# A rotary embedding kernel: another order of the first small loads on the SyncE and ScalarE queues

## The chip, the cores and the metric

The kernel runs on one core of one Trainium2 chip. The metric is device time in microseconds (us) of one execution; lower is better. The kernel before was timed three times.

## The reference

`x` has the shape (8, 2048, 16, 64): batch, sequence, heads, head dimension, in float32. `cos` and `sin` have the shape (2048, 32), one row for each place in the sequence, and hold for all batches and heads. Each head's 64 values are taken as two halves and rotated:

```python
x1 = x[..., :head_dim // 2]
x2 = x[..., head_dim // 2:]
out1 = x1 * cos - x2 * sin
out2 = x1 * sin + x2 * cos
return concatenate([out1, out2], axis=-1)      # float32
```

In bytes: 67.1 MB of `x` are read, 67.1 MB are written, and sine and cosine are 256 KB each.

## The kernel before

**Layout.** The 2048 places are spread over 128 partitions, 16 in a row on each (`J` = 16), so that one partition has for each batch 16 rows of 1024 values (`W` = 16 heads x 64). Work is done in float16: loads on the GpSimd queue turn float32 into float16 on the way, and stores on it turn it back. `buf` holds five batches (`SLOTS` = 5), and batch b lives in slot b modulo 5.

**Queues.** Nearly all traffic goes through one queue, that of GpSimd (POOL), by the helper `queue` (line 57), which ties each transfer behind the one before it in program order. The calls from line 100 on are thus the order of the queue: load of batch 0 without its first two rows, store of the first row of batch 0, load of batches 1 and 2, load of batches 3 and 4, store of the rest of batch 0, store of 1 and 2, load of 5, load of 6 and 7, and so on. A store waits for VectorE's last step on its rows; a load into a used slot waits for the store that empties it.

**The opening.** SyncE (SP) asks for sine (line 50, `sin_f`). ScalarE (ACT) asks for cosine (line 51, `cos_f`) and then for the *head*: the first two rows of batch 0, 1 MB in float32 (line 52). The head isn't converted on its way; it lands in float32 in the space of slot 4. Then ScalarE works in program order:

- lines 101 and 102: two conversions of sine to float16, one of them with a minus sign (`sin_h`), ahead of which the table load of ScalarE runs;
- line 103: the conversion of cosine (`cos_h`);
- line 96, twice (`narrow_head`): the head's two rows to float16.

**The rotation.** `rotate` is three VectorE instructions: the swapped halves times sine into `v` (line 87), the values times cosine in place (line 91), and their sum (line 93). The first call takes the first row alone (128 x 1024 values), the second the other 15 rows of batch 0, and the others a whole batch each (128 x 16384).

**The end.** The last two rows of batch 7 are turned to float32 on ScalarE (line 127) and stored from SyncE (line 128), behind a part of the batch's store.

Of the kernel before, what the change touches and what calls it, by code (L numbers as in the profile page):

```python
# [1 line left out]

# [4 lines left out]


@with_exitstack  # L10
def kernel(
    ctx: ExitStack,
    tc: tile.TileContext,
    x: bass.AP,
    cos: bass.AP,
    sin: bass.AP,
    out: bass.AP,
):
    nc = tc.nc
    f16 = mybir.dt.float16  # L20
    f32 = mybir.dt.float32

    B, S, H, D = x.shape
    Dh = D // 2
    P = nc.NUM_PARTITIONS
    J = S // P
    SLOTS = 5
    JA = 2
    JE = 2
    JF = 1  # L30

    pool = ctx.enter_context(tc.tile_pool(name="rope", bufs=1))
    buf = pool.tile([P, SLOTS, J, H, D], f16)
    v = pool.tile([P, J, H, D], f16)
    sin_f = pool.tile([P, J, Dh], f32)
    cos_f = pool.tile([P, J, Dh], f32)
    cos_h = pool.tile([P, J, Dh], f16)
    sin_h = pool.tile([P, J, D], f16)

    def words(slot, rows):  # L40
        flat = buf[:, slot, 0 : 2 * rows].rearrange("p j h d -> p (j h d)")
        return flat.bitcast(f32)

    head = words(SLOTS - 1, JA)
    tail = words(SLOTS - 2, JE)
    rows_in = x.rearrange("b (p j) h d -> p b (j h d)", j=J)
    rows_out = out.rearrange("b (p j) h d -> p b (j h d)", j=J)
    W = H * D

    nc.sync.dma_start(out=sin_f, in_=sin.rearrange("(p j) d -> p j d", j=J))  # L50
    nc.scalar.dma_start(out=cos_f, in_=cos.rearrange("(p j) d -> p j d", j=J))  # L51
    nc.scalar.dma_start(out=head, in_=rows_in[:, 0, 0 : JA * W])

    ring = []

    def queue(dst, src):
        dma = nc.gpsimd.dma_start(out=dst, in_=src)  # L57
        if ring:
            tc.add_manual_dep(
                dma.ins,  # L60
                ring[-1].ins.name,
                mybir.DependencyInfo(mybir.DependencyClass.NoSync, mybir.DependencyReason.DATA),
                reason="order of the ring",
            )
        ring.append(dma)
        return dma

    def part(b, n, j0, j1):
        s = b % SLOTS
        return buf[:, s : s + n, j0:j1].rearrange("p n j h d -> p n (j h d)")  # L70

    def load(b, n=1, j0=0):
        return queue(part(b, n, j0, J), rows_in[:, b : b + n, j0 * W : J * W])

    def store(b, n=1, j0=0, j1=J):
        return queue(rows_out[:, b : b + n, j0 * W : j1 * W], part(b, n, j0, j1))

    def rotate(b, j0=0, j1=J):
        n = j1 - j0
        js = slice(j0, j1)  # L80
        xt = buf[:, b % SLOTS, js]
        vt = v[:, js]
        shape = [P, n, H, 2, Dh]
        sin_b = sin_h[:, js, :].rearrange("p j (e d) -> p j e d", e=2).unsqueeze(2).to_broadcast(shape)
        cos_b = cos_h[:, js, :].unsqueeze(2).to_broadcast([P, n, 2 * H, Dh])
        xe = xt.rearrange("p j h (e d) -> p j h e d", e=2)
        nc.vector.tensor_mul(  # L87
            out=vt.rearrange("p j h (e d) -> p j h e d", e=2), in0=xe[:, :, :, ::-1, :], in1=sin_b
        )
        xw = xt.rearrange("p j h (e d) -> p j (h e) d", d=Dh)  # L90
        nc.vector.tensor_mul(out=xw, in0=xw, in1=cos_b)  # L91
        xa = xt.rearrange("p j h d -> p (j h d)")
        nc.vector.tensor_add(out=xa, in0=xa, in1=vt.rearrange("p j h d -> p (j h d)"))  # L93

    def narrow_head(j0, j1):
        nc.scalar.copy(  # L96
            out=buf[:, 0, j0:j1].rearrange("p j h d -> p (j h d)"), in_=head[:, j0 * W : j1 * W]
        )

    load(0, j0=JA)  # L100
    nc.scalar.copy(out=sin_h[:, :, Dh:D], in_=sin_f)  # L101
    nc.scalar.mul(out=sin_h[:, :, 0:Dh], in_=sin_f, mul=-1.0)  # L102
    nc.scalar.copy(out=cos_h, in_=cos_f)  # L103
    narrow_head(0, JF)
    narrow_head(JF, JA)
    rotate(0, 0, JF)
    store(0, j1=JF)
    load(1, 2)
    load(3, 2)
    rotate(0, JF, J)  # L110
    store(0, j0=JF)
    rotate(1)
    rotate(2)
    store(1, 2)
    load(5)
    load(6, 2)
    rotate(3)
    rotate(4)
    store(3, 2)
    rotate(5)  # L120
    rotate(6)
    store(5, 2)
    rotate(7)
    gate = store(7, j1=9)
    store(7, j0=9, j1=J - JE)

    nc.scalar.copy(out=tail, in_=buf[:, (B - 1) % SLOTS, J - JE : J].rearrange("p j h d -> p (j h d)"))  # L127
    end = nc.sync.dma_start(out=rows_out[:, B - 1, (J - JE) * W : J * W], in_=tail)
    tc.add_manual_dep(
        end.ins,  # L130
        gate.ins.name,
        mybir.DependencyInfo(mybir.DependencyClass.Sync, mybir.DependencyReason.DATA),
        reason="the last rows go out behind this part",
    )


# [1 line left out]
_INS = ['x', 'cos', 'sin']  # L138
_OUTS = [((8, 2048, 16, 64), 'float32')]


# [23 lines left out]
```

## Time and profile before

| | us |
|---|---|
| median of 3 runs (316.36 to 316.49) | 316.48 |
| the profiled execution, its own time | 316.32 |
| its span in the profile | 314.6 |
| VectorE (DVE) busy | 209.1 (66%) |
| ScalarE (ACT) busy | 6.8 (2%) |
| GpSimd (POOL) busy | 7.9 (3%) |
| HBM read and written over the span | 428 GB/s |
| head: from its issue at 1.15 to its landing | 12.1 |
| load of batch 0: from its issue at 1.25 to its landing | 22.6 |

The span is the stretch from the first to the last instruction that the profiler recorded; the execution's own time has some 1.7 us more around it. All places in time below are counted from the span's start. DVE, ACT, POOL and SP are the engines; a "q" behind a name (ACTq, SPq) is the engine's sequencer, which issues the transfers. q0 is GpSimd's queue, q1 SyncE's and q10 ScalarE's; all of them are served by the same 16 DMA engines. "Idle before" is time in which an engine waited, and the releaser is what ended it. A row of the timeline gives start and duration, then engine, line, operation, what is written and what is read, and in brackets the wait ahead of it.

### The profile page before, as it was taken

To read this page: it belongs to the slowest core of one execution; us is meant where nothing else is said; L and a number is where in the kernel's file an instruction comes from. 1 tells how busy PE (TensorE), PEld (TensorE's weight loads), DVE (VectorE), ACT (ScalarE), POOL (GpSimd) and SP (SyncE) were. 2 spreads that over 40 slices of the span, in tenths; PEclk is the share of its full clock that TensorE was granted. 3 is DMA by queue.
4 is the path that set the end of the run, shared out by engine and by line. 5 is a ranking of instruction groups with operands and counts; after the bars stand their busy time and mean duration, and the time that the engine had idled before them with its cause. 6 is when DMAs were issued, how large, how long until landed. Compare 5 with 4: busy or idle time off the path is not lost.

```text
span 314.6 us, 113 instructions
## 1 busy us (share of the span) xinstructions
DVE 209.1 (66%) x27; ACT 6.8 (2%) x7; POOL 7.9 (3%) x16
## 2 busy tenths in 40 slices
DVE  0109991089999999999994399903999999200000
ACT  3200000000000000000000000000000000200000
POOL 1020000000000000000000000000000000100000
DMA  7989999999999899999999999999999999999998
GB/s 230 261 193 249 267 200 200 200 267 200 200 200 325 375 500 400 400 400 533 400 200 221 246 200 200 250 217 333 400 517 417 400 400 525 408 400 400 433 425 342
DMA packets 3072, 101.71 MB, mean 323 GB/s; under 512 B 256, under 2 KB 256, under 8 KB 640
## 3 DMA queue, kind: packets, MB, share of 16 engines
q0 software_dynamic: 2496, 99.09, 98.1%
q1 hardware_dynamic: 288, 1.31, 1.2%
q10 hardware_dynamic: 288, 1.31, 1.0%
HBM read 67.63 MB, written 67.11 MB: 428 GB/s over the span
## 4 chain that ended last, share of the span: by engine, by line
DVE 59%; DMA 19%; another core or an unknown queue 7%; ACT 1%; issue 0%; POOL 0%; ACTq 0%; DVEq 0%
DVE v L87 20%; DVE buf L91 20%; DVE buf L93 20%; DMA buf<-in_x_dram 19%; ACT buf L127 1%; ACT buf L96 0%; POOL out_dram L57 0%; ACTq L51 0%; DVEq L87 0%
## 5 line engine op out<-in xcount | busy, mean ns | idle before, releaser
L87 DVE TENSOR_TENSOR v<-buf,sin_h 128x16384 f16<-128x16384 f16 (+2 forms) x9 | 69.7, 7744 | 59.7 <-DMA buf<-in_x_dram 45.3
L91 DVE TENSOR_TENSOR buf<-buf,cos_h 128x16384 f16<-128x16384 f16 (+2 forms) x9 | 69.7, 7744 | 0.3
L93 DVE TENSOR_TENSOR buf<-buf,v 128x16384 f16<-128x16384 f16 (+2 forms) x9 | 69.7, 7744 | 0.3
L57 POOL DMA_DIRECT2D out_dram<-buf x7 | 4.3, 620 | 219.7 <-DVE buf L93 219.7
L127 ACT CAST buf<-buf 128x2048 f32<-128x2048 f16 x1 | 1.9, 1897 | 254.2 <-DVE buf L93 254.2
L57 POOL DMA_DIRECT2D buf<-in_x_dram x5 | 3.4, 679 | 43.0 <-DMA out_dram<-buf 42.2
L96 ACT CAST buf<-buf 128x1024 f16<-128x1024 f32 x2 | 2.0, 1042 | 7.2 <-DMA buf<-in_x_dram 7.2
L101 ACT ACT_TABLE_LOAD x1 | 1.3, 1283 | 1.7 <-PEq L149 1.7
L101 ACT CAST sin_h<-sin_f 128x512 f16<-128x512 f32 x1 | 0.6, 617 | 1.5 <-DMA sin_f<-in_sin_dram 1.5
L102 ACT ACTIVATE sin_h<-sin_f 128x512 f16<-128x512 f32 x1 | 0.6, 624 | 0.0
L103 ACT CAST cos_h<-cos_f 128x512 f16<-128x512 f32 x1 | 0.6, 601 | 0.0
L149 POOL MEMSET const-float32-0.0<- 128x1 f32 x1 | 0.1, 99 | 0.2 <-issue 0.2
L149 POOL MEMSET const-bfloat16-1.0<- 128x1 bf16 x1 | 0.1, 102 | 0.0
L149 POOL MEMSET const-float32-1.0<- 128x1 f32 x1 | 0.1, 99 | 0.0
L149 POOL MEMSET const-uint8-127<- 128x1 uint8 x1 | 0.1, 99 | 0.0
## 6 DMA issues: line engine op xcount, KB each, us to landing
buf<-in_x_dram POOLq DMA_DIRECT2D x3, 8192.0 KB, 57.1
out_dram<-buf POOLq DMA_DIRECT2D x1, 7680.0 KB, 71.7
out_dram<-buf POOLq DMA_DIRECT2D x1, 4608.0 KB, 35.5
buf<-in_x_dram POOLq DMA_DIRECT2D x1, 4096.0 KB, 57.3
buf<-in_x_dram POOLq DMA_DIRECT2D x1, 3584.0 KB, 22.6
out_dram<-buf POOLq DMA_DIRECT2D x1, 2560.0 KB, 41.0
buf<-in_x_dram ACTq DMA_DIRECT2D x1, 1024.0 KB, 12.1
out_dram<-buf SPq DMA_DIRECT2D x1, 1024.0 KB, 8.4
```

What stands on the lines that cost most here:

```text
L57: dma = nc.gpsimd.dma_start(out=dst, in_=src)
L87: nc.vector.tensor_mul(out=vt.rearrange("p j h (e d) -> p j h e d", e=2), in0=xe[:, :, :, ::-1, :], in1=sin_b)
L91: nc.vector.tensor_mul(out=xw, in0=xw, in1=cos_b)
L93: nc.vector.tensor_add(out=xa, in0=xa, in1=vt.rearrange("p j h d -> p (j h d)"))
L96: nc.scalar.copy(out=buf[:, 0, j0:j1].rearrange("p j h d -> p (j h d)"), in_=head[:, j0 * W : j1 * W])
L101: nc.scalar.copy(out=sin_h[:, :, Dh:D], in_=sin_f)
L102: nc.scalar.mul(out=sin_h[:, :, 0:Dh], in_=sin_f, mul=-1.0)
L103: nc.scalar.copy(out=cos_h, in_=cos_f)
L127: nc.scalar.copy(out=tail, in_=buf[:, (B - 1) % SLOTS, J - JE : J].rearrange("p j h d -> p (j h d)"))
L149: nc = _bacc.Bacc("TRN2", target_bir_lowering=False, num_devices=1)
```

## The change

SyncE asks for sine and then for the head. VectorE clears one word of a new small tile, ScalarE copies it to the word beside it, and ScalarE's issue of cosine waits by semaphore for that copy. The copy is now ScalarE's first arithmetic instruction, so the table load comes ahead of it. All that follows is as it was.

```diff
     nc.sync.dma_start(out=sin_f, in_=sin.rearrange("(p j) d -> p j d", j=J))
-    nc.scalar.dma_start(out=cos_f, in_=cos.rearrange("(p j) d -> p j d", j=J))
-    nc.scalar.dma_start(out=head, in_=rows_in[:, 0, 0 : JA * W])
+    nc.sync.dma_start(out=head, in_=rows_in[:, 0, 0 : JA * W])
+    word = pool.tile([P, 2], f32)
+    nc.vector.memset(word[:, 0:1], 0.0)
+    warm = nc.scalar.copy(out=word[:, 1:2], in_=word[:, 0:1])
+    cosine = nc.scalar.dma_start(out=cos_f, in_=cos.rearrange("(p j) d -> p j d", j=J))
+    tc.add_manual_dep(
+        cosine.ins,
+        warm.ins.name,
+        mybir.DependencyInfo(mybir.DependencyClass.Sync, mybir.DependencyReason.DATA),
+        reason="the first rows are asked for ahead of cosine",
+    )
```

## The prediction

> **What bounds the kernel now.** I read the page first, then the chain of waits, then the timeline and the DMA view of the first microseconds, and last the trace's list of DMA packets, which has the queue, size, start and duration of each one (numbers called "packet" below are from that list, in microseconds from the span's start). From the page:
>
> ```profile
> span 314.6 us, 113 instructions
> ...
> DMA  7989999999999899999999999999999999999998
> ...
> q0 software_dynamic: 2496, 99.09, 98.1%
> q1 hardware_dynamic: 288, 1.31, 1.2%
> q10 hardware_dynamic: 288, 1.31, 1.0%
> ```
>
> The reader is to see that the packets of the three queues fill 100.3% of 16 engines' span. By the packet list the engines have no gap of more than 0.04 us from 2.8 us, when the slow first packets of sine are through, to 313.3. Every kind of packet runs at one pace: 57,344 bytes read for a first-load row take 2.13 us, 65,536 bytes stored take 2.45 us, both 26.8 to 26.9 GB/s an engine. So the transfers are the bound, and the end moves only if the engines begin earlier, carry less, or run dry somewhere. The chain of waits says something else:
>
> ```profile
> 1.15 12.08 DMA buf<-in_x_dram
> ...
> 16.79 0.47 POOL out_dram L57
> ...
> 17.31 46.40 DMA buf<-in_x_dram
> ```
>
> It goes through the head rows, which land at 13.24, to the load issued at 17.31. But that load needs 41.9 us for its 8,192 KB at the 200 GB/s of the page's slices and shows 46.40: it stood behind the first load, whose last packet ended at 23.5. The timeline of the opening, in order of time:
>
> ```profile
> 0.73 0.39 ACTq L51 DMA_DIRECT2D cos_f<-in_cos_dram  x1
> 0.74 0.38 SPq L50 DMA_DIRECT2D sin_f<-in_sin_dram  x1
> 1.15 0.47 ACTq L52 DMA_DIRECT2D buf<-in_x_dram  x1
> 1.25 0.67 POOL L57 DMA_DIRECT2D buf<-in_x_dram  x1 [0.80 <-PEq L160]
> 1.65 1.28 ACT L101 ACT_TABLE_LOAD   x1 [1.65 <-PEq L149]
> 4.45 0.62 ACT L101 CAST sin_h<-sin_f 128x512 f16<-128x512 f32 x1 [1.52 <-DMA sin_f<-in_sin_dram]
> 4.98 0.62 ACT L102 ACTIVATE sin_h<-sin_f 128x512 f16<-128x512 f32 x1
> 5.51 0.60 ACT L103 CAST cos_h<-cos_f 128x512 f16<-128x512 f32 x1
> 13.26 1.99 ACT L96 CAST buf<-buf 128x1024 f16<-128x1024 f32 x2 [7.15 <-DMA buf<-in_x_dram]
> ...
> 16.79 0.53 POOL L57 DMA_DIRECT2D out_dram<-buf  x1 [14.88 <-DVE buf L93]
> 17.31 1.43 POOL L57 DMA_DIRECT2D buf<-in_x_dram  x2
> 23.94 8.16 DVE L87 TENSOR_TENSOR v<-buf,sin_h 128x15360 f16<-128x15360 f16 x1 [7.46 <-DMA buf<-in_x_dram]
> ```
>
> What matters here is the slack: the first store is issued at 16.79, and its packets could not begin before 23.27, when the first load's last ones were through. The DMA view of 0 to 14 us, in 40 slices of 0.35 us:
>
> ```profile
> GB/s 0 0 0 0 0 94 0 146 374 404 398 527 492 468 374 398 1299 82 0 0 0 0 328 1358 0 0 0 0 0 374 1311 0 0 0 0 0 1311 0 0 0
> ```
>
> A packet counts in the slice where it starts. Sine, cosine and six of each engine's eight head rows go up to slice 15. The first load's first row starts in slice 16 (packet: 5.71), and from then on each engine takes one row of it (2.11 us from start to next start) and one head row (0.32) in turn: slices 23, 30, 37. The last two head rows and the closing four-byte packet thus waited for three rows of the load, and that made the landing 13.24. Packets alternate singly between the queues.
>
> **The change part by part.** The profiled execution is the base: 316.32 us, of which the span is 314.6 and 1.7 lie around it; the median of the three runs, 316.48, is 0.16 above it, and the forecast is made against that median.
>
> *Bytes.* None are added or taken away: 0.
>
> *Start of the engines.* Sine stays first on SP at 0.74 and its first packet at 1.76; the first packets take 0.84 us as they do now. Head's issue moves from behind cosine on ACT (1.15) to behind sine on SP (0.74 + 0.38, again about 1.15). At the 1.02 from issue to first packet that sine shows, it is ready at 2.2, before sine's eight packets an engine are done at 3.2 (2.6 + 7 x 0.083). No gap: 0.
>
> *The wait.* The clear of one word on VectorE (nearest row: MEMSET 128x1 on POOL, 0.10; VectorE is idle until 14.34) is hidden behind the table load. That load is no longer behind two issues, so it runs from 0.73 to 2.01. The copy's cost comes from CAST rows: 0.617 for 512 elements and 1.044 for 1024 leave 0.19 for one. With 0.03 to 0.08 for a semaphore (14.31 to 14.34; 305.18 to 305.26), cosine is issued at about 2.3 in place of 0.73, and its first packet comes at 3.3 to 3.5. Behind the waiting issue on ACT stand the sine casts (they wait for sine until 3.6 anyway), the cosine cast and both head casts; VectorE waits for those, then POOL's store.
>
> *Who lands when.* Until 5.7, when the first load's packets begin, the same 3.1 us of each engine's work is done, dealt out otherwise: sine 0.66, then head rows of 0.309 and cosine rows of 0.083 in turn. Head rows begin at 3.2 and cosine after the first or second of them, so each pair costs 0.39: (5.7 - 3.5) / 0.39 gives 5 to 6 cosine rows and 6 to 7 head rows by then. With n cosine rows left, cosine lands at 5.8 + (n + 1) x 2.13 + 0.5 to 1.0 (the head and cosine rows between, and the 0.34 from last packet to landing). n = 2 gives 13.1 and n = 3 gives 15.4. Head lands at 11.0 with seven rows done, 13.3 with six. The slowest engine decides, so I take cosine 13.1, range 11.0 to 15.4. **Cosine becomes the late one**, as the cast of cosine stands ahead of the head casts.
>
> *Store and next loads.* From cosine's landing: 0.02, cast 0.53 (pitch 4.98 to 5.51), and 3.53 as now from first head cast to store (13.26 to 16.79). The store is issued at 13.1 + 4.08 = 17.2, at worst of the range 19.5, against 16.79. The cover is the 23.27 at which the queue runs empty. How long a POOL issue takes to its first packet is bounded by two rows: 4.46 for the first load (1.25 to 5.71), and at most 3.45 for the store issued at 116.42, whose packets came at 119.87 as the queue came free. I take 3.45, being a store in mid-kernel as this is: 17.2 + 3.45 = 20.7, and 22.95 at 19.5; both in time. With 4.46 the worst is 24.0, a gap of 0.7. The loads of line 57 follow 0.52 behind the store, whose own packets last 1.5 us an engine: covered too. Below nothing: no earlier landing can gain, as no gap is there to be filled.
>
> Sum: 0 + 0 + 0, and up to 0.7: 316.5, own range 316.2 to 317.2.
>
> **The Trainium skill** in one place speaks against the change: "ScalarE: Activation LUTs", What ACT_TABLE_LOAD costs, gives about 1283 ns for the load and about 1380 ns of drain besides. The trace agrees with the first (1.28); the second it can't show, since ScalarE waited for sine. By it, cosine would be issued at about 3.7; that is the first rival. In another place, "DMA: Bandwidth & Descriptors", Queues, rings and completion order, an engine is said to drain a packet of some 9 to 17 descriptors from one queue before it turns to the next. By that rule cosine's eight rows would go out in one turn near 4 us and the first rival would fall; the single head rows between load rows in slices 23 and 30 speak against it here.
>
> **Rivals.** First, slower: *cosine comes too late and the software queue runs dry.* The gap after the table load was 1.52 (2.93 to 4.45); sine ended it, but it may hide a settling time of the load. If all of it is kept, the copy runs at 3.53, cosine is issued at 3.75, its packets begin at 4.8, only 2 or 3 rows go before 5.7, and five or six are left: landing at 19.6 to 21.7, store issued at 23.7 to 25.8. With 1.02 from issue to packet (sine's row, the shortest) the engines stand idle 1.4 to 3.5 us, with 3.45 it is 3.9 to 6.0: 317.9 to 322.5. It decides from four rows left, a landing of 17.6 (store 21.7, gap 0 to 1.9; 316.5 to 318.4), that is from cosine packets beginning about 4.0. For it: this gap, and that nothing in the trace shows an operation right behind a table load. Against it: no instruction stands in that gap, and sine's landing at 4.43 explains its end. Chance 0.21 with all that makes it slower by over 0.2%.
>
> Second, faster: *the chain is right.* Head lands a round or more earlier (2.4 us), the store and the load of 46.40 move with it: 314.1. Against it: the load was behind 6 us of other packets, and cosine's cast stands before the head casts. Chance 0.07, with smaller gains.
>
> Third, *the wait does nothing:* were the copy over before the table load, cosine would go at about 1.1 and the old order of landings would return: 316.5, inside the forecast. Chance 0.04 of the 0.72 for no change.
>
> **How the numbers follow.** 0.2% (0.63 us) is about what a measurement of this kernel can tell from no change; the three runs lie within 0.13. No change 0.72, slower 0.21, faster 0.07. The range goes from 316.1 (the spread, and a little for a shorter opening) over the own range into the first rival, to the middle of its cheaper end, 1.4 to 3.5, at 2.4: 318.8. Left out are the dearer end (about 0.08) and true gains (0.06).
>
> **What would show it.** Right: cosine issued near 2.3; in the DMA view a first-load row still near 5.7 and pulses every 2.4 us; the cosine cast no longer at 5.5 but behind 11; the store issued at 17 to 19.5; the DVE row of 23.94 and the load landing at 63.7 unmoved; DMA full from 2.8 to 313. Wrong: a store issue after 20 us, an empty slice near 23.5 to 27, and everything behind it later by the same amount; or a first-load landing earlier than 23.5, which would mean that the opening does have something to save.

## The result, and the profile after

The changed kernel takes 323.83 us (median of 5 runs, 323.69 to 324.04), against 316.42 for the kernel before in the same session: ratio 1.0235, 95% interval 1.022 to 1.025. It is slower by 7.4 us, outside the range of 316.1 to 318.8. The profiled execution took 323.92 us; its span is 7.6 us longer than that of before. From the page of the changed kernel:

```profile
span 322.1 us, 115 instructions
...
DMA  9885999999999999999999999999999999999998
```

A slice is 8.05 us here. The fourth, 24.2 to 32.2 us, has the engines busy for half of it; in the kernel before that stretch was full. The rest looks as it did. The timeline of the changed kernel shows how it came to that:

```profile
0.73 1.28 ACT L54 ACT_TABLE_LOAD   x1 [0.73 <-PEq L158]
...
1.15 0.42 SPq L51 DMA_DIRECT2D buf<-in_x_dram  x1
...
2.03 0.19 ACT L54 COPY word<-word 128x1 f32<-128x1 f32 x1
2.25 0.37 ACTq L55 DMA_DIRECT2D cos_f<-in_cos_dram  x1
...
23.88 0.62 ACT L112 CAST cos_h<-cos_f 128x512 f16<-128x512 f32 x1 [19.18 <-DMA cos_f<-in_cos_dram]
...
27.93 0.53 POOL L66 DMA_DIRECT2D out_dram<-buf  x1 [26.02 <-DVE buf L102]
```

Cosine is asked for at 2.25, as foretold, and its cast runs at 23.88 instead of 5.51. The store of the first row follows at 27.93 instead of 16.79, and the two loads behind it in GpSimd's queue as late. The DMA view of 0 to 14 us in slices of 0.35:

```profile
GB/s 0 0 0 0 0 23 176 392 533 351 374 468 538 421 632 866 164 0 0 0 94 825 603 0 0 0 0 135 1106 164 0 0 0 0 1147 257 0 0 0 0
```

By the list of DMA packets, sine and 123 of the head's 128 rows go out up to slice 15, not one cosine row among them. The first load's rows begin at 5.12 to 5.75; the first cosine rows go out at 7.50 to 7.87 (slices 21 and 22), after the first of those rows. From then on each engine takes one cosine row and one row of the load in turn, eight times: cosine lands at 23.85. The first load's last packets are through at 23.39, and then the engines have nothing. The stretches of the changed kernel around that (length, busy time of DVE, ACT and POOL with the number of instructions, granted clock, DMA share, GB/s; a packet counts where it starts):

```profile
24.00:27.00 3.00, 1.46 (x3) 2.39 (x3) 0.00 (x0) 1.00 0.00 0
27.00:29.00 2.00, 2.00 (x2) 0.00 (x0) 1.07 (x2) 1.00 0.00 0
29.00:30.00 1.00, 1.00 (x1) 0.00 (x0) 0.89 (x2) 1.00 1.23 430
```

The last landings come 7.6 us later. Where that arises is seen from the end of each transfer's last packets in the two traces (us):

| GpSimd's queue | before | after | difference |
|---|---|---|---|
| first load | 23.55 | 23.39 | -0.16 |
| store of the first row | 24.80 | 30.44 | +5.64 |
| load of batches 1 and 2 | 63.43 | 70.11 | +6.69 |
| load of batches 3 and 4 | 102.05 | 109.66 | +7.61 |
| all later ones | | | +7.61 |

The empty stretch itself gives 5.8. The next step is 1.05: after the store of the first row, nine engines wait 0.1 to 0.8 us more for the next load's first row, and those first rows take 2.7 to 3.5 us, not 2.43. The last 0.92 is in the final rows of the load of batches 3 and 4, near 106 us, which take 0.82 us longer on all 16 engines.

### The profile page after: what moved, and what is told of

Same layout as the page of the kernel before. It is cut to its first block, busy times and chain, and to the rows that moved or that the text cites. A ratio compares the mean times of both kernels' runs of the same rounds, so it can differ in the third digit from the quotient of the medians.

```text
span 322.1 us, 115 instructions
## 1 busy us (share of the span) xinstructions
DVE 209.1 (65%) x28; ACT 7.0 (2%) x8; POOL 7.9 (2%) x16
## 2 busy tenths in 40 slices
DMA packets 3072, 101.71 MB, mean 316 GB/s; under 512 B 256, under 2 KB 256, under 8 KB 640
## 4 chain that ended last, share of the span: by engine, by line
DVE 57%; DMA 20%; another core or an unknown queue 7%; ACT 2%; issue 0%; POOL 0%; DVEq 0%
DVE v L96 19%; DVE buf L100 19%; DVE buf L102 19%; DMA buf<-in_x_dram 13%; DMA cos_f<-in_cos_dram 7%; ACT buf L136 1%; ACT L54 0%; ACT buf L105 0%; ACT cos_h L112 0%; POOL out_dram L66 0%; ACT word L54 0%; DVEq L96 0%
```

## The experiments

All start from the changed kernel. "Theory A" is that cosine's late arrival at the engines, and nothing else of the change, makes the loss: each cosine row that is left when the first load's rows begin pays one of those rows. A1 to A4 in the expectations are guesses at why cosine's first packet came so long after its issue; A1 is that rows of other transfers, which the engines have taken on already, delay it.

**The wait taken out.**

```diff
-    word = ...; memset; warm = copy; cosine = nc.scalar.dma_start(out=cos_f, ...); wait of cosine for warm
+    nc.scalar.dma_start(out=cos_f, in_=cos.rearrange("(p j) d -> p j d", j=J))
```

> SyncE asks for sine and the head as in the changed kernel; ScalarE asks for cosine at once, with no word, copy or wait. Theory A (the late issue of cosine is the cause: its rows come to the DMA engines when the first load is already there, and each row then pays one row of that load, 2.2 us): cosine and sine rows alternate from 1.8 us, cosine lands before 5 us, head at 11 to 13.5, the store of the first row is issued before 17, the queue never runs empty, 316.4 us (316.1 to 316.8). Theory B (the head in SyncE's queue is the cause: ScalarE's transfer is held up behind it whenever it was asked for): cosine's first packet still comes after 5 us, cosine lands after 15, and the time is over 319.

Measured: 316.41 us against 316.40, ratio 1.0001 (0.9992 to 1.001). Its timeline:

```profile
0.73 0.40 ACTq L52 DMA_DIRECT2D cos_f<-in_cos_dram  x1
...
5.21 0.60 ACT L103 CAST cos_h<-cos_f 128x512 f16<-128x512 f32 x1
...
16.67 0.53 POOL L57 DMA_DIRECT2D out_dram<-buf  x1 [14.77 <-DVE buf L93]
```

Head on SyncE costs nothing and brings nothing: the store is issued 0.12 us earlier than before, and the time is the same. Theory B is out, and with the head on SyncE the whole loss hangs on the late issue of cosine.

**The wait alone.** Head goes back to ScalarE, behind cosine in the program; the wait stays.

```diff
-    nc.sync.dma_start(out=head, in_=rows_in[:, 0, 0 : JA * W])
...
+    nc.scalar.dma_start(out=head, in_=rows_in[:, 0, 0 : JA * W])   # after cosine
```

> The other part alone: ScalarE asks for cosine behind its table load and the copy, and then for the head, as the kernel before does; SyncE asks for sine only. Cosine is issued near 2.25 us as in the changed kernel. Theory A1 (an issue finds the engines at once when they have little queued, and 3 to 5 us later only when they have rows of another queue): sine is through at 3.1, so cosine's first packet comes at 3.3 to 3.5, head follows from 4.1, three or four of its rows are through when the first load begins near 5.3, and four or five are left: head lands at 17 to 20, the store is issued at 20.5 to 23.6, 316.5 to 320 us. Theory A2 (an issue at 2.25 takes some 5 us whatever is queued): first packet near 7.5, head behind cosine until 26, store at 30, 324 to 326 us.

Measured: 322.24 us, ratio 1.0185 (1.017 to 1.02). It doesn't answer what it was made for: the compiled order has the head's issue first on ScalarE (0.74) and cosine's behind the first sine cast, at 6.02. So both theories stay open here. Its timeline:

```profile
6.02 0.34 ACTq L54 DMA_DIRECT2D cos_f<-in_cos_dram  x1
...
24.05 0.62 ACT L112 CAST cos_h<-cos_f 128x512 f16<-128x512 f32 x1 [13.68 <-DMA cos_f<-in_cos_dram]
...
26.43 0.53 POOL L66 DMA_DIRECT2D out_dram<-buf  x1 [24.52 <-DVE buf L102]
```

Cosine lands at 24.03, the store is issued at 26.43, and the queue runs dry as in the changed kernel. It is thus one more case of a late cosine, with the head out of SyncE's queue.

**No wait, but cosine last in SyncE's queue.**

```diff
     nc.sync.dma_start(out=head, ...)
-    word = ...; warm = ...; cosine = nc.scalar.dma_start(out=cos_f, ...); wait
+    nc.sync.dma_start(out=cos_f, in_=cos.rearrange("(p j) d -> p j d", j=J))
```

> All three on SyncE: sine, head, cosine, issued by 2 us, no copy and no wait. Theory A says that not the wait as such costs, but the count of cosine rows left when the first load begins: they stand behind the head's rows in one ring, head ends near 5.4 us, so seven or eight cosine rows are left, each pays one row of the load, cosine lands at 21 to 24, store at 25 to 28, 321 to 324 us. A rival (only the delay from issue to first packet of the late issue costs): cosine is ready by 3 us and lands before 10, 316.4 us.

Measured: 322.12 us, ratio 1.0181 (1.0166 to 1.0196). Its timeline:

```profile
1.64 0.42 SPq L52 DMA_DIRECT2D cos_f<-in_cos_dram  x1
...
23.64 0.62 ACT L103 CAST cos_h<-cos_f 128x512 f16<-128x512 f32 x1 [14.54 <-DMA cos_f<-in_cos_dram]
...
26.02 0.53 POOL L57 DMA_DIRECT2D out_dram<-buf  x1 [24.11 <-DVE buf L93]
```

Here cosine waits for no table load and is asked for 0.6 us earlier, yet it lands as late: its rows stand behind the head's in one queue, all eight are left on each engine at 5.2 us, and each pays a row of the load. So it is the order in which the rows reach the engines that costs.

**The loads freed of the late store.** The load of batches 1 and 2 goes ahead of the first row's store in GpSimd's queue.

```diff
-    store(0, j1=JF)
     load(1, 2)
+    store(0, j1=JF)
```

> The changed kernel with one step moved: the load of batches 1 and 2 stands ahead of the store of the first row in the GpSimd queue, so that it doesn't wait for cosine. Cosine is as late as in the changed kernel (lands near 24, store issued near 28). If the whole loss is the queue that ran empty from 23.4 to 29.0 us and the slow rows behind that, the time is that of the kernel before, 316.4 us (316.1 to 317). If something else of the change costs (a slower pace of the transfers, the slow rows near 106 us, the longer opening), some of the 7.4 us stays, over 317.5.

Measured: 316.81 us, ratio 1.0013 (1.0004 to 1.0023). Cosine is as late as in the changed kernel (cast at 23.90, store issued at 27.94), but the stretches that were empty are full (a packet counts where it starts):

```profile
24.00:27.00 3.00, 1.43 (x3) 2.42 (x3) 0.00 (x0) 1.00 0.81 175
27.00:29.00 2.00, 2.00 (x2) 0.00 (x0) 1.06 (x2) 1.00 1.22 262
```

Of 7.4 us, 7.0 are gone. The dry queue, with what follows from it, is thus nearly the whole loss; this run doesn't part the empty stretch from the slow rows behind it. The group of longer rows near 106 us is gone; one of 16 rows near 60 us is longer by 0.38 on average, about as much as the 0.4 us that stay.

**Short packets.** The first load in seven pieces.

```diff
-    load(0, j0=JA)
+    for j in range(JA, J, 2):
+        queue(part(0, 1, j, j + 2), rows_in[:, 0:1, j * W : (j + 2) * W])
```

> The changed kernel with its first load split into seven, each of two of the 14 rows of a partition, so that one packet takes 0.31 us and not 2.13. Theory A (each cosine row left pays one packet of the load): cosine lands at 8 to 10.5 us, not 23.9, the store of the first row is issued at 12 to 15, the queue does not run dry, 316.3 to 317.3 us. A rival (cosine waits until the first load is through, whatever its packets are): lands near 24, 323 us or more.

Measured: 316.61 us, ratio 1.0006 (0.9996 to 1.0015). Its timeline:

```profile
10.08 0.62 ACT L113 CAST cos_h<-cos_f 128x512 f16<-128x512 f32 x1 [5.51 <-DMA cos_f<-in_cos_dram]
```

With the issue as late as in the changed kernel (2.25), cosine lands at 10.05, the store is issued at 14.11, and nothing runs dry. By the packet list its rows begin at 5.99 to 6.63 and are through at 9.45: eight rows at some 0.4 us each, one packet of the load and one of cosine. That makes the price "one packet of the load for each row" a measured one.

**Why the first cosine row came at 7.5.** Two runs take away what is queued beside it: in one, head and first load both wait; in the other the first load alone (it waits for cosine).

> What delays cosine's first packet, asked for near 2.25 us as in the changed kernel: here no other transfer is queued then but sine (through at 3.1 us), since the head waits for the first sine cast and the first load of GpSimd's queue waits for cosine. Theory A1 (an issue that meets rows of other transfers in the engines waits for them): cosine's first packet near 3.3 us, 1.0 behind its issue, as sine's. Theory A2 (ScalarE's issue behind its table load and copy is slow in itself): first packet at 5 to 7.5 us here too. The time is that of the kernel before plus the opening's new gaps, 317 to 321 us by either.

> The changed kernel, except that the first load of GpSimd's queue waits for cosine; head and cosine are asked for as in the changed kernel. If the head's rows alone hold cosine up (rows that the engines have taken on ahead of it, A1), cosine's first packet comes when the head's rows are through, 5.1 to 5.5 us, not between them. If it was the first load of GpSimd's queue, or its preparation, that held cosine up (A3), cosine's rows go between the head's from 3.3 us on. Time 318 to 322 us by either, since the first load starts late.

Measured: 319.44 and 319.26 us, each in a single run. The issue is at 2.25 in both, as their timelines show, the first two lines from the one with nothing beside it, the others from the one with the head:

```profile
2.25 0.36 ACTq L54 DMA_DIRECT2D cos_f<-in_cos_dram  x1
...
5.06 0.62 ACT L124 CAST cos_h<-cos_f 128x512 f16<-128x512 f32 x1 [0.43 <-DMA cos_f<-in_cos_dram]
```

```profile
2.25 0.36 ACTq L55 DMA_DIRECT2D cos_f<-in_cos_dram  x1
...
6.51 0.62 ACT L118 CAST cos_h<-cos_f 128x512 f16<-128x512 f32 x1 [1.97 <-DMA cos_f<-in_cos_dram]
```

By the packet lists, cosine's first packet comes at 3.56 with nothing but sine around it, 1.3 us behind the issue (1.0 was expected); with the head's rows queued it comes at 5.13, 2.9 behind, when the engine has the last head row out, and never between two of them. (A wait for the head's rows and a wait of some 3 us end at the same place here, so this run alone can't tell them apart.) A2 and A3 are out: neither ScalarE's late issue in itself nor the first load held cosine up, but what the engines had queued.

**A number of packets or a time?** Three kernels, each run once, with the wait's word and copy gone. Cosine is asked for behind the head casts, when only the first load's packets are in the engines; the load goes in pieces of two rows of a partition, seven, and one.

```diff
     narrow_head(0, JF)
-    narrow_head(JF, JA)
+    last = narrow_head(JF, JA)
+    cosine = nc.scalar.dma_start(out=cos_f, ...)      # waits by semaphore for last
+    nc.scalar.copy(out=cos_h, in_=cos_f)
```

> As the run before with short packets, but cosine is asked for on ScalarE behind the two head casts (the word, its copy and the wait for it are gone), near 9 to 11 us, when nothing but the first load's packets of 0.31 us is in the engines. If any rows that the engines have taken on delay a new issue (A1), its first packet comes 3 to 5 us behind its issue; if only a transfer of the other hardware queue does (A4), 1.0 to 1.4 us. The time is within 1 us of the kernel before unless cosine lands after 17.

> As the run that asks for cosine behind the head casts, but the first load goes in two halves of seven rows of a partition, so that a packet takes 1.07 us and not 0.31. There cosine's first packet came 3.4 us behind its issue, after some 8 to 11 packets. If a new issue waits for a number of packets that the engines have taken on, it is 8 to 11 us here, or until the load is through near 23; if it waits a time that does not depend on the packets, 3.4 to 4.5 us.

> The same with fourteen pieces of one row, packets of 0.155 us. A number of packets gives 1.3 to 2.2 us from issue to first packet; a fixed time gives 3.4.

| packets of the load | cosine issued | first packet | between | time |
|---|---|---|---|---|
| 0.155 us | 8.18 | 11.71 | 3.5 | 317.04 |
| 0.31 us | 8.24 | 11.64 | 3.4 | 317.45 |
| 1.07 us | 9.02 | 12.87 | 3.9 | 320.02 |

The issue and what followed from it in the run with packets of 1.07 us:

```profile
9.02 0.36 ACTq L105 DMA_DIRECT2D cos_f<-in_cos_dram  x1
21.95 0.62 ACT L112 CAST cos_h<-cos_f 128x512 f16<-128x512 f32 x1 [12.95 <-DMA cos_f<-in_cos_dram]
...
24.31 0.54 POOL L56 DMA_DIRECT2D out_dram<-buf  x1 [21.86 <-DVE buf L92]
```

Packets seven times as long don't change the wait by more than half of one of them. The run with the wait alone adds a fourth point: amid packets of 2.13 us its first cosine packet came at 9.62, 3.6 us behind the issue. So it isn't a number of packets: a time of some 3.4 us fits, and then the rest of the packet under way. A fixed amount of data would fit as well, as the engines move data at one pace in all four. A1 holds for these loads, A4 (only another hardware queue's transfer delays) doesn't. What in the engines takes that time isn't settled.

Cosine lands at 14.6, 15.8 and 21.9 (in the order of the table), and only the last, with its store at 24.31, runs the queue dry. The other two are 0.7 and 1.05 us above the kernel before all the same, the second just outside the 1 us that was expected. By the packet lists their slowest engine ends the store of the first row at 25.51 and 25.93, against 24.80 in the kernel before, so the time is lost ahead of that; why isn't shown.

## Why the prediction was wrong, point by point

- **The bound** was read rightly: transfers alone, so that nothing could be gained and only an empty stretch could lose. The bytes are the same (101.71 MB), and with the wait taken out the time is that of before (ratio 1.0001).
- **The wait** was sized rightly: table load at 0.73, copy 0.19, issue at 2.25 against "about 2.3". The Trainium skill's drain of about 1380 ns behind a table load ("ScalarE: Activation LUTs", What ACT_TABLE_LOAD costs) isn't paid here: the copy starts 0.02 us behind the load's end.
- **The failed step is "its first packet comes at 3.3 to 3.5".** It took the 1.02 us of sine's issue, which met idle engines, for an issue that meets engines with the head's rows queued. Measured: 7.50. With the 2.9 us behind the head alone, or the 3.4 to 3.9 amid load packets, cosine would be ready at 5.1 to 6.2; the first load's rows began at 5.12 to 5.75, most of them ahead of the 5.7 that was assumed. By these figures cosine had to let the row under way pass, until 7.5. So no cosine row was through when the load began, not five or six.
- **The step that goes on from it** held. Each row left pays one row of the load, and with n = 8 in place of 2 or 3 cosine lands when the load ends, at 23.85. (The sum's n = 3 gives 15.3 and not 15.4; nothing hangs on that.) The term of 4.08 from landing to store is exact: 23.85 + 4.08 = 27.93.
- **Issue to first packet of the store** was taken as 3.45; on idle engines it is 1.10 (27.93 to 29.03). It made the gap smaller, but the restart that the sum didn't have put 2.0 us on top (rows of 2.7 to 3.5 us, the later group near 106).
- **The first rival** was the right mechanism at the right place (cosine late, store late, the queue dry), with the wrong reason for the delay and a chance of only 0.21. Its dearest case leaves the queue empty for 6.0 us, near the 5.6 that passed between 23.39 and 29.03, but by luck: two cosine rows too few (a store at 25.8, not 27.93) and 3.45 in place of 1.10 us to the store's first packet cancel. What its 322.5 lacks is mainly the 2.0 us of restart and later slow rows.

The profile of before had the warning. Cosine's own row there is one: issued at 0.73, it had its first packet at 2.62, 1.9 us behind, with only sine's rows beside it. SyncE's store of the last rows is issued under full load, and the DMA view of 303 to 315 us (slices of 0.3) shows its 8 KB rows:

```profile
305.26 0.35 SPq L128 DMA_DIRECT2D out_dram<-buf  x1
```

```profile
GB/s 1597 369 0 0 0 1024 68 819 273 0 1024 68 819 273 0 1024 68 819 273 0 1024 68 751 341 0 382 410 437 437 437 437 437 437 82 0 0 0 0 0 0
```

The even flow near 437 GB/s from slice 25 on is that store; its first packet is at 310.56, 5.3 us behind the issue. On every engine it comes right behind GpSimd's last row, so it doesn't fit the 3.4 to 3.9 us of the loads; why it waited longer isn't shown. The first load's 4.46 was another such row. All three are nearer to an issue into busy engines than sine's at 0.74.

## What to carry to other kernels

Take the time from a DMA's issue to its first packet from a row of the trace with the same load on the engines: a row from an idle start is no estimate for an issue into busy ones. Where queues alternate packet by packet, a small transfer that comes behind a large one pays a large packet for each of its own; ask for the small ones first, or make the large one's packets short. In a kernel bound by transfers, look for what could let the one long queue run empty: an early store that waits for a small operand, ahead of loads that wait for nothing, is such a place. Putting the loads first took 7.0 of the 7.4 us away here.

## What the runs showed of the hardware

- From issue to first packet of a transfer of SyncE or ScalarE: 1.0 to 1.3 us with little queued, 1.9 for cosine beside sine's first packets (kernel before), 2.9 behind the head's rows, 3.4 to 3.9 amid the load's packets whether these take 0.155 or 2.13 us, and 5.3 for SyncE's store at the end of the kernel before. For GpSimd's queue 1.10 on idle engines against 4.46 in the opening of the kernel before.
- After an empty stretch the next load's first rows take 2.7 to 3.5 us, not 2.43.
- In the four traces with a queue that ran dry before the load of batches 1 and 2, one row on each engine some 76 us behind the restart is 0.6 to 0.8 us longer on average (near 106 us in the changed kernel, 102 to 105 in the others). Without that, groups longer by 0.2 to 0.4 on average were seen at other places in four runs (near 21 us with the wait taken out, near 60 with the loads first, at 21 to 24 in the two in which the first load waits), and none in the kernel before. Their cause stays open.
